# A hybrid decoder step on one core: u chunks beside the gate weights, 18 rather than 10

## The chip, the cores and the metric

One core of a Trainium2 chip runs the whole program. Its engines work side by side and wait for each other by semaphores: the matrix engine (PE), the vector engine (DVE), the activation engine (ACT), GpSimd (POOL), and SyncE (SP), which issues most transfers. The metric is the device time of one execution in microseconds; less is better.

## The reference

Two layers, a prompt of 256 tokens with 16 meta tokens ahead, and 8 samples of 4 tokens. Layer 0 mixes with RWKV-7, layer 1 with a Mamba-2 state-space part; behind each stands the same expert mixer, which the change touches most:

```python
q = (xt @ w_q).reshape(T, P_HEADS, 2, P_QDIM // 2)
s = jnp.einsum('thzd,zhkd->thzk', q, sub_keys)
sv, si = lax.top_k(s, 16)                    # two halves of a key
cand = sv[:, :, 0, :, None] + sv[:, :, 1, None, :]
top_s, pos = lax.top_k(cand.reshape(T, 8, 256), 16)
gate = jax.nn.softmax(top_s, axis=-1)        # 8 heads x 16 experts of 16384
act = gelu(einsum('td,ted->te', x_blk, u_tab[eidx]))
out = einsum('te,ted->td', gate * act, v_tab[eidx])
```

All is in float32. The outputs are the two groups' activations and the states of both mixers.

## The kernel before, in words

**The mixer (peer).** For the 256 prompt tokens the experts aren't gathered: all 16384 are computed, in 128 chunks of 128 experts, and a gate weight that is zero for an expert that wasn't chosen leaves the right ones. (The 48 or 32 other tokens do gather their rows, by indirect transfers that POOL issues in the v loop.) The tile G holds, for chunk b and token t, first gelu(u x) and then its product with the gate weight. Four stages follow each other in each layer:

1. *Queries and scores* for the keys, in tiles ti = 1, 2 (128 tokens each) and 0 (the gathered ones).
2. *The u loop*, 56 chunks (B0). s_chunk() fetches 128 x 1024 weights on SP's queue, splits them into a high part (a cast on ACT, L279) and a low part (a subtraction on POOL, L284, or on DVE, L286), and PE multiplies 24 times (mm3: L305, L306, L308) into the PSUM tile psc; ACT applies gelu (L1080) into G. Meanwhile DVE selects the best keys in topk(0), topk(1), topk(2). The table AFTER says behind which chunk the three last steps of each tile stand: exps() on ACT (L1019), gates() on DVE (L1022 to L1024), and finish(). finish() transposes the two key numbers and the gate of each choice on PE (ptk, L1029) and ACT copies them into sel (L1032).
3. *The gate stage*: 64 groups of four tokens. onehots() builds from sel two one-hot tiles oa and ob for each token, on DVE, ACT and POOL by the letters of WA; PE multiplies them (pwt, L1135), which gives the gate weights of all 16384 experts for that token. DVE multiplies them into the 56 chunks that G has (L1136), and ACT copies those of the other 72 chunks into G (L1137). Among the groups stand NF = 10 further u chunks, whose gelu goes into a scratch tile hs; at the end ten multiplies (L1139) bring hs into G.
4. *The v loop*: for each b the product of G's chunk with the v rows, 12 products into four accumulators acc (L1288), after a split of both into high and low parts (gh and glo, whi and wlo). In between the 62 u chunks that are left, each with one multiply of its own (L1252).

**What sets the order.** Both mixers stand in a block whose instructions a scheduler of the compiler lists by a simulated timeline: on each engine it may move an instruction ahead of others that it doesn't depend on, so a u chunk of stage 3 can stand far ahead of its place in the text. Calls of keep_in_program_order (in finish(), exps() and the start of gates()) hold an instruction at its place. On the chip each engine then works through its list in that order.

**The state-space part** begins with prenorm(): xh on ACT (L337), xl on DVE (L339), the squares (L315, L319), and a first projection on PE between. Ahead of it two weight tiles are split, their low halves on POOL (load_w with leng = 8), and L1340 casts a mask on DVE.

Some settings: W1 = 3 buffers of each one-hot tile; two each of whi and wlo; PSUM banks o = 4, s = 2, m = 2.

Of the kernel before, what the change touches and what calls it, by code (L numbers as in the profile page):

```python
# [23 lines left out]
F32 = mybir.dt.float32  # L24
F32R = mybir.dt.float32r
# [3 lines left out]
AF = mybir.ActivationFunctionType  # L29
# [8 lines left out]
KB = 8  # L38
# [28 lines left out]
def chain(*gens):  # L67
    for g in gens:
        yield from g
# [157 lines left out]
class K:  # L227
# [104 lines left out]

    def prenorm(self, out, h, g, xh, xl, sq, rr, tag, mid):

        nc = self.nc
        for k in range(KB):
            x = nc.scalar.activation(xh[:, k], h[:, k], AF.Copy, scale=self.vec(g, k))  # L337
            self.tc.keep_in_program_order(x)
            nc.vector.scalar_tensor_tensor(xl[:, k], h[:, k], self.vec(g, k), xh[:, k].bitcast(F32), op0=ALU.mult, op1=ALU.subtract)  # L339
        self.rmsnorm(out, h, g, sq, None, tag, rr, mid)  # L340
        return rr[1]
# [509 lines left out]
    def peer(self, l, ng):  # L851

        nc, tc, a, C, V = self.nc, self.tc, self.a, self.C, self.nc.vector
        mm = nc.tensor.matmul
        B0 = 56
        NF = 10
        W1 = 3
        FH = 10
        FL = 4
# [6 lines left out]
        raws = {i: self.fetch(a[f"wq{l}"][i]) for i in range(3)}  # L866
# [4 lines left out]
        G = gp.tile([128, 128, 256], F32, name="G")  # L871
        Gf = G.rearrange("p b t -> p (b t)")
        xh = gp.tile([128, KB, T], F32R, name="xh")
        xl = gp.tile([128, KB, T], F32R, name="xl")
# [64 lines left out]
        late = {}  # L939
# [135 lines left out]
        def s_chunk(b, dst, heng=None, leng=None, tag="s"):  # L1075

            w = self.load_w(a[f"u{l}"][b], heng=heng, leng=leng)
            p = self.bank([128, 256], "psc", tag)
            self.mm3(p, w, (xh[:, :, 48:T], xl[:, :, 48:T]))
            nc.scalar.activation(dst, p, AF.Gelu)  # L1080

# [7 lines left out]

        AFTER = ((14, 16, 55), (29, 31, 39), (46, 46, 52))  # L1090
        for b in range(B0):
# [31 lines left out]

        nf = 0
        nxt = onehots(0)
        for t0 in range(0, 256, 4):
            if nf < NF and t0 * NF >= nf * 256:
                s_chunk(B0 + nf, hs[:, nf * 256:nf * 256 + 256], heng=None if nf % 10 < FH else V, leng=FL)
                nf += 1
            oa, ob = nxt  # L1130
            if t0 < 252:
                nxt = onehots(t0 + 4)
            pw = self.bank([128, 4, 128], "pwt", "mo"[t0 // 4 % 3 > 0])
            for j in range(4):
                mm(pw[:, j], lhsT=oa[:, j], rhs=ob[:, j], start=True, stop=True)  # L1135
            V.tensor_mul(G[:, 0:B0, t0:t0 + 4], G[:, 0:B0, t0:t0 + 4], pw[:, :, 0:B0].rearrange("p t b -> p b t"))  # L1136
            nc.scalar.copy(G[:, B0:, t0:t0 + 4], pw[:, :, B0:].rearrange("p t b -> p b t"))  # L1137
        for i in range(NF):
            V.tensor_mul(G[:, B0 + i], G[:, B0 + i], hs[:, i * 256:i * 256 + 256])  # L1139

# [95 lines left out]
        def slot():  # L1236
# [6 lines left out]
            return 4 * r  # L1243

        ggen = chain(gather_u(range(ng)), gather())
        nleft = 128 - B0 - NF
        done = 0
        for b in range(128):
# [34 lines left out]
            todo = [(i, g, w) for g, w in ((gh, vhf), (gl, vhf), (gh, vlf)) for i in range(4)]  # L1283
            if b == 127:
                todo.sort(key=lambda x: x[0])
            for i, g, w in todo:
# [16 lines left out]
        for i, pt in enumerate(self.gpt):  # L1303
            hk = self.h[:, 4 * i:4 * i + 4, 0:16 * ng].rearrange("p k (g t) -> p k g t", t=16)
            V.tensor_add(hk, hk, pt.rearrange("p k (g t) -> p k g t", t=32)[:, :, 0:ng, 0:16])
        for i in range(4):
            ot = gview(100 + 2 * i, (128, 512))
            if i % 2:
                V.tensor_copy(ot, acc[i])
            else:  # L1310
                nc.scalar.copy(ot, acc[i])
            pt = self.bank([128, 4, 128], "pot", "s")
            for j in range(4):
                mm(pt[:, j], lhsT=ot[:, j * 128:(j + 1) * 128], rhs=C["eye"], is_transpose=True, start=True, stop=True)
            t0 = 48 + i // 2 * 128
            hk = self.h[:, i % 2 * 4:i % 2 * 4 + 4, t0:t0 + 128]
            V.tensor_add(hk, hk, pt)
# [3 lines left out]
    def mamba(self):  # L1321
# [17 lines left out]
        mk = pp.tile([128, 3, 128], BF, name="mk")  # L1339
        V.tensor_copy(mk[:, 2], C["eye"])  # L1340
        self.psum(i=2, G=2, f=2, t=2)
# [8 lines left out]
        done = [0]  # L1350
        pre = {b: self.load_w(a["win"][b], leng=LE, raw=raws[b]) for b in (40, 32)}
        xn = ep.tile([128, KB, T], F32, name="xn", tag="E")
        rr = ep.tile([128, 2, T], F32, name="rr", tag="E")

        def proj(blk):
# [7 lines left out]
            if done[0] == NU:  # L1363
                with tc.high_priority(offset=200):
                    for k in range(KB):
# [6 lines left out]
        ri = self.prenorm(xn, self.h, "nm1", xh, xl, ep.tile([128, KB, T], F32, name="sq", tag="E"), (rr[:, 0], rr[:, 1]), "t",  # L1372
                          lambda: first.append(proj(40)))
        gp = st.enter_context(tc.tile_pool(name="mg", bufs=2, reuse_waits="tile"))
# [34 lines left out]
        def decays(dp):  # L1409
# [310 lines left out]
```

## Time and profile before

| what | us |
|---|---|
| median of 3 runs (lowest, highest) | 2630.28 (2629.93, 2636.83) |
| the profiled execution; its span | 2634.19; 2632.3 |
| busy PE / DVE / ACT / POOL in the span | 2478 / 1899 / 1254 / 1008 |
| layer 0: u loop, gate stage, v loop (from, to) | 485-678, 678-785, 785-1328 |
| layer 1: u loop, gate stage, v loop | 1760-1967, 1967-2075, 2075-2622 |

In the rows of the profile an instruction is named by its line, engine, operation, and output<-inputs; the brackets give how long the engine stood idle before it and what ended that. PE's products are pipelined, so the time from one start to the next is their price, not the length printed. The rows of windows give the stretch, then busy time and count for PE, PE's weight loads, DVE, ACT and POOL (or for the engine asked alone), then the granted PE clock (1.00 is full), the share of the DMA engines, and GB/s.

### The profile page before, as it was taken

To read this page: it belongs to the slowest core of one execution; us is meant where nothing else is said; L and a number is where in the kernel's file an instruction comes from. 1 tells how busy PE (TensorE), PEld (TensorE's weight loads), DVE (VectorE), ACT (ScalarE), POOL (GpSimd) and SP (SyncE) were. 2 spreads that over 40 slices of the span, in tenths; PEclk is the share of its full clock that TensorE was granted. 3 is DMA by queue.
4 is the path that set the end of the run, shared out by engine and by line. 5 is a ranking of instruction groups with operands and counts; after the bars stand their busy time and mean duration, and the time that the engine had idled before them with its cause. 6 is when DMAs were issued, how large, how long until landed. Compare 5 with 4: busy or idle time off the path is not lost. (4 is left out here: it accounts for less than half of the span.)

```text
span 2632.3 us, 47459 instructions
## 1 busy us (share of the span) xinstructions
PE 2477.9 (94%) x18281; PEld 2137.4 (81%) x18281; DVE 1898.8 (72%) x3724; ACT 1253.6 (48%) x2384; POOL 1008.2 (38%) x863
## 2 busy tenths in 40 slices
PE   7999999996989999999978988999889899999998
PEld 4677768996978888888864886989789788888886
DVE  5355556797695678788784887769949756776777
ACT  3322223453784444444456543335448644444444
POOL 4111110495980233533146555117769401223210
PEclk9999999998999999999989999999989999999999
DMA  3111115453416788888732443555543267787774
GB/s 142 51 45 50 47 55 170 141 183 121 134 40 215 250 312 309 299 306 299 273 110 80 156 164 118 160 177 154 168 122 98 84 213 257 255 285 268 261 265 157
DMA packets 125858, 460.34 MB, mean 175 GB/s; under 512 B 14816, under 2 KB 15744, under 8 KB 122432
## 3 DMA queue, kind: packets, MB, share of 16 engines
q1 hardware_dynamic: 99488, 360.75, 42.1%
q0 software_dynamic: 26144, 96.56, 10.2%
q8 instruction: 144, 2.36, 0.4%
q14 instruction: 82, 0.67, 0.1%
HBM read 440.70 MB, written 16.56 MB: 174 GB/s over the span
## 5 line engine op out<-in xcount | busy, mean ns | idle before, releaser
L279 ACT CAST whi<-wraw 128x1024 fp32r<-128x1024 f32 (+1 forms) x619 | 642.1, 1038 | 870.7 <-PE acc L1288 312.9
L286 DVE TENSOR_TENSOR wlo<-wraw,whi 128x1024 fp32r<-128x1024 f32 (+1 forms) x493 | 593.7, 1204 | 397.2 <-ACT whi L279 339.6
L305 PE MATMUL psc<-xh,whi 128*128 128x256 f32 x2048 | 506.6, 285 | 3.1 <-ACT h L1080 2.6
L306 PE MATMUL psc<-xl,whi 128*128 128x256 f32 x2048 | 504.8, 283 | 0.0
L284 POOL TENSOR_TENSOR wlo<-wraw,whi 128x1024 fp32r<-128x1024 f32 (+1 forms) x150 | 355.1, 2374 | 176.5 <-ACT whi L279 91.0
L305 PEld LDWEIGHTS psc<-xh,whi 128*128 128x128 f32 x2048 | 388.0, 189 | 10.0 <-ACT h L1080 3.1
L306 PEld LDWEIGHTS psc<-xl,whi 128*128 128x128 f32 x2048 | 388.6, 190 | 5.5
L1066 POOL DMA_INDIRECT G<-in_un,gi x80 | 114.5, 1432 | 468.5 <-DVE glo L286 304.6
L1288 PE MATMUL acc<-whi,glo 128*128 128x512 f32 x1024 | 285.1, 399 | 6.7 <-DVE glo L286 6.7
L308 PE MATMUL psc<-xh,wlo 128*128 128x256 f32 x2048 | 290.3, 283 | 0.0
L1288 PE MATMUL acc<-whi,gh 128*128 128x512 f32 x1024 | 283.9, 398 | 1.9 <-ACT gh L279 1.0
L1288 PE MATMUL acc<-wlo,gh 128*128 128x512 f32 x1024 | 281.8, 397 | 0.0
L308 PEld LDWEIGHTS psc<-xh,wlo 128*128 128x128 f32 x2048 | 263.0, 188 | 0.5 <-issue 0.3
L1288 PEld LDWEIGHTS acc<-whi,glo 128*128 128x128 f32 x1024 | 193.8, 190 | 54.8 <-DVE glo L286 7.6
L1288 PEld LDWEIGHTS acc<-wlo,gh 128*128 128x128 f32 x1024 | 192.7, 189 | 47.8 <-DVE wlo L286 1.3
L1163 POOL DMA_INDIRECT G<-in_v,gi x80 | 117.0, 1463 | 298.2 <-DVE G L1158 163.8
L1288 PEld LDWEIGHTS acc<-whi,gh 128*128 128x128 f32 x1024 | 185.0, 189 | 40.3 <-ACT whi L279 1.6
L1135 PE MATMUL pwt<-ob,oa 128*128 128x128 f32 x1024 | 144.8, 282 | 11.6 <-DVE ob L1109 7.8
L1135 PEld LDWEIGHTS pwt<-ob,oa 128*128 128x128 f32 x1024 | 127.8, 191 | 23.2 <-issue 19.3
L305 PE MATMUL pi<-xh,whi 128*128 128x304 f32 (+1 forms) x328 | 102.5, 331 | 11.7 <-ACT xh L279 3.7
L286 DVE TENSOR_TENSOR glo<-G,gh 128x256 fp32r<-128x256 f32 x256 | 106.9, 419 | 2.7 <-ACT gh L279 2.7
L279 ACT CAST gh<-G 128x256 fp32r<-128x256 f32 x256 | 101.8, 399 | 11.7 <-PE acc L1288 11.6
(484 smaller groups left out, 4444.0 us busy)
## 6 DMA issues: line engine op xcount, KB each, us to landing
wraw<-in_u SPq DMA_DIRECT2D x256, 512.0 KB
wraw<-in_v SPq DMA_DIRECT2D x256, 512.0 KB
wraw<-in_win SPq DMA_DIRECT2D x41, 512.0 KB
wraw<-in_wq SPq DMA_DIRECT2D x32, 512.0 KB
wraw<-in_rkv SPq DMA_DIRECT2D x24, 512.0 KB
h<-in_ssm SPq DMA_DIRECT2D x8, 1024.0 KB
out_sssm<-h POOLq DMA_DIRECT2D x8, 1024.0 KB
wraw<-in_wo SPq DMA_DIRECT2D x8, 512.0 KB
```

Source lines behind the costliest of these rows:

```text
L279: self.nc.scalar.copy(hi, x)
L284: self.nc.gpsimd.tensor_sub(lo[:, :n], x[:, :n], hi[:, :n].bitcast(F32))
L286: self.nc.vector.tensor_sub(lo[:, n:], x[:, n:], hi[:, n:].bitcast(F32))
L305: nc.tensor.matmul(ps, lhsT=whi[:, k], rhs=xhi[:, x0 + k], start=start and k == 0, stop=False)
L306: nc.tensor.matmul(ps, lhsT=whi[:, k], rhs=xlo[:, x0 + k], start=False, stop=False)
L308: nc.tensor.matmul(ps, lhsT=wlo[:, k], rhs=xhi[:, x0 + k], start=False, stop=stop and k == kb - 1)
L1066: nc.gpsimd.indirect_dma_start(out=rows, out_offset=None, in_=a[f"un{l}"], in_offset=bass.IndirectOffsetOnAxis(ap=gi[:, 0, g, m:m + 1], ax ...
L1135: mm(pw[:, j], lhsT=oa[:, j], rhs=ob[:, j], start=True, stop=True)
L1163: nc.gpsimd.indirect_dma_start(out=rows, out_offset=None, in_=vrows, in_offset=bass.IndirectOffsetOnAxis(ap=gi[:, 1, g, m:m + 1], axis=0))
L1288: mm(acc[i], lhsT=g[:, t0:t0 + 128], rhs=w[:, d0:d0 + 512], start=b == 0 and g is gh and w is vhf, stop=b == 127 and w is vlf)
```

## The change

- **NF is 18.** Chunks 56 to 73 stand in the gate stage and 54 are left for the v loop. A chunk that stands before token t0 writes gelu for the tokens below t1 = t0 + 8 into hs, and for the others straight into its place in G (two activations). When the loop comes to t1, a DVE multiply (the join, L1141) brings the hs part into G, and from there on the chunk is one of the nb columns that DVE multiplies in each group (L1149); ACT copies the rest (L1150).
- **AFTER** moves finish(1) from chunk 39 to 52, exps(2) and gates(2) from 46 to 45, and finish(2) from 52 to 55.
- **The end of the v loop**: the products of b = 126 are kept and issued with those of b = 127, sorted by accumulator, in layer 0 in the order 0, 2, 1, 3.
- **The start of the state-space part**: the two low halves go to DVE, behind xl (lows()), and the mask's cast moves to a later place on DVE.

```diff
-    def prenorm(self, out, h, g, xh, xl, sq, rr, tag, mid):
+    def prenorm(self, out, h, g, xh, xl, sq, rr, tag, mid, then=None):
...
+        if then is not None:
+            then()
         self.rmsnorm(out, h, g, sq, None, tag, rr, mid)
...
-        NF = 10
+        NF = 18
...
-            nc.scalar.activation(dst, p, AF.Gelu)
+            for d, c in dst if isinstance(dst, tuple) else ((dst, slice(0, 256)),):
+                if c.start < c.stop:
+                    nc.scalar.activation(d, p[:, c], AF.Gelu)
...
-        AFTER = ((14, 16, 55), (29, 31, 39), (46, 46, 52))
+        AFTER = ((14, 16, 55), (29, 31, 52), (45, 45, 55))
...
         for t0 in range(0, 256, 4):
             if nf < NF and t0 * NF >= nf * 256:
-                s_chunk(B0 + nf, hs[:, nf * 256:nf * 256 + 256], heng=None if nf % 10 < FH else V, leng=FL)
+                t1 = min(t0 + 8, 256)
+                t = hs[:, nf % 10 * 256:nf % 10 * 256 + t1]
+                s_chunk(B0 + nf, ((t, slice(0, t1)), (G[:, B0 + nf, t1:], slice(t1, 256))), leng=FL)
+                late.append((t1, B0 + nf, t))
                 nf += 1
+            if late and late[0][0] <= t0:
+                t1, b, t = late.pop(0)
+                V.tensor_mul(G[:, b, 0:t1], G[:, b, 0:t1], t)
+                nb = b + 1
...
-            V.tensor_mul(G[:, 0:B0, t0:t0 + 4], G[:, 0:B0, t0:t0 + 4], pw[:, :, 0:B0].rearrange("p t b -> p b t"))
-            nc.scalar.copy(G[:, B0:, t0:t0 + 4], pw[:, :, B0:].rearrange("p t b -> p b t"))
-        for i in range(NF):
-            V.tensor_mul(G[:, B0 + i], G[:, B0 + i], hs[:, i * 256:i * 256 + 256])
+            V.tensor_mul(G[:, 0:nb, t0:t0 + 4], G[:, 0:nb, t0:t0 + 4], pw[:, :, 0:nb].rearrange("p t b -> p b t"))
+            nc.scalar.copy(G[:, nb:, t0:t0 + 4], pw[:, :, nb:].rearrange("p t b -> p b t"))
+        for t1, b, t in late:
+            V.tensor_mul(G[:, b, 0:t1], G[:, b, 0:t1], t)
...
-            if b == 127:
-                todo.sort(key=lambda x: x[0])
+            if b == 126:
+                kept = todo
+                todo = []
+            elif b == 127:
+                todo = sorted(kept + todo, key=lambda x: ORD.index(x[0]))
...
-        pre = {b: self.load_w(a["win"][b], leng=LE, raw=raws[b]) for b in (40, 32)}
+        pre = {}
+        for b in (40, 32):
+            pre[b] = tuple(self.wp.tile([128, KB, 128], F32R, name=n, tag=n) for n in ("whi", "wlo"))
+            nc.scalar.copy(pre[b][0], raws[b])
+        def lows():
+            for b in (40, 32):
+                tc.keep_in_program_order(V.tensor_sub(pre[b][1], raws[b], pre[b][0].bitcast(F32)))
```

**How the order moves.** Line numbers of the changed kernel are up to 15 higher. First ACT in the u loop of layer 0, around the first copy of sel (L1032, now L1033). Before it stands behind the gelu of chunk 39:

```order
L279 CAST whi<-wraw 128x1024
L1080 ACTIVATE G<-psc 128x256
L1032 COPY sel<-ptk 128x3x128
L1114 ACTIVATE oa<-cp,sel 128x128 x5
L1115 ACTIVATE oa<-oa,sel 128x128 x3
L279 CAST whi<-wraw 128x1024
```

and now behind that of chunk 52, with the second copy close to it:

```order
L1083 ACTIVATE G<-psc 128x256
L1033 COPY sel<-ptk 128x3x128
L1117 ACTIVATE oa<-cp,sel 128x128 x5
L1118 ACTIVATE oa<-oa,sel 128x128 x3
L279 CAST whi<-wraw 128x1024
L1118 ACTIVATE oa<-oa,sel 128x128 x2
L1083 ACTIVATE G<-psc 128x256
L279 CAST whi<-wraw 128x1024
L1083 ACTIVATE G<-psc 128x256
L279 CAST whi<-wraw 128x1024
```

Thirteen chunks, their casts and their gelus, moved ahead of the copy, as on PE ahead of the transposes.

Next DVE at the end of the gate stage and the first b of the v loop. Before:

```order
L1118 TENSOR_SCALAR ob<-cp,sel 128x128 x2
L1120 TENSOR_SCALAR oa<-cp,sel 128x128
L1136 TENSOR_TENSOR G<-G,pwt 128x56x4 x3
L286 TENSOR_TENSOR wlo<-wraw,whi 128x1024
L1139 TENSOR_TENSOR G<-G,h 128x256 x10
L286 TENSOR_TENSOR glo<-G,gh 128x256 x3
```

and now:

```order
L1121 TENSOR_SCALAR ob<-cp,sel 128x128 x2
L1123 TENSOR_SCALAR oa<-cp,sel 128x128
L1141 TENSOR_TENSOR G<-G,h 128x236
L1149 TENSOR_TENSOR G<-G,pwt 128x73x4 x2
L1149 TENSOR_TENSOR G<-G,pwt 128x74x4
L1141 TENSOR_TENSOR G<-G,h 128x252
L1266 TENSOR_TENSOR G<-G,h 128x256
L286 TENSOR_TENSOR glo<-G,gh 128x256 x3
```

The ten multiplies of 256 columns ahead of the three lower halves glo are gone; one join and one multiply of a v-loop chunk stand there, and the other joins stand among the groups, each some 3.5 groups behind the last.

More of the change, by code (lines that the diff above doesn't have):

```diff
@@ L855, in peer @@
         B0 = 56
-        NF = 10
+        NF = 18
         W1 = 3
-        FH = 10
         FL = 4
@@ L1124, in peer @@
         nf = 0
+        nb = B0
+        late = []
         nxt = onehots(0)
@@ L1243, in slot @@
             return 4 * r
+        ORD = (0, 1, 2, 3) if last else (0, 2, 1, 3)
         ggen = chain(gather_u(range(ng)), gather())
@@ L1305, in peer @@
             V.tensor_add(hk, hk, pt.rearrange("p k (g t) -> p k g t", t=32)[:, :, 0:ng, 0:16])
-        for i in range(4):
+        for n, i in enumerate(ORD):
             ot = gview(100 + 2 * i, (128, 512))
-            if i % 2:
+            if n % 2:
                 V.tensor_copy(ot, acc[i])
@@ L1339, in mamba @@
         mk = pp.tile([128, 3, 128], BF, name="mk")
-        V.tensor_copy(mk[:, 2], C["eye"])
         self.psum(i=2, G=2, f=2, t=2)
@@ L1372, in mamba @@
         ri = self.prenorm(xn, self.h, "nm1", xh, xl, ep.tile([128, KB, T], F32, name="sq", tag="E"), (rr[:, 0], rr[:, 1]), "t",
-                          lambda: first.append(proj(40)))
+                          lambda: first.append(proj(40)), lows)
         gp = st.enter_context(tc.tile_pool(name="mg", bufs=2, reuse_waits="tile"))
@@ L1418, in decays @@
             tc.keep_in_program_order(V.tensor_copy(mk[:, 0:2], nm))
+            V.tensor_copy(mk[:, 2], C["eye"])
             p = xs
```

## The prediction

> **What bounds the kernel now.** I read first which waits stop the matrix engine (PE), in the view of waits for PE alone (who waited, for whom, us in total, times, longest).
>
> ```profile
> PE ptk L1029 <- DVE G L1024: 20.5, 2, 10.2
> PE ptk L1029 <- DVE G L1016: 19.3, 2, 9.8
> ...
> PE acc L1288 <- DVE glo L286: 6.7, 2, 3.4
> ```
>
> Three rows hold 46.5 us, at the same two places in both layers: the transposes ptk of finish(), and the start of the v loop. The timeline of PE shows the first place in layer 0, then in layer 1.
>
> ```profile
> 607.37 0.27 PE L1029 MATMUL ptk<-c,G 128*128 128x128 f32 x1
> 617.43 0.47 PE L1029 MATMUL ptk<-c,G 128*128 128x128 f32 x1 [9.80 <-DVE G L1016]
> 628.15 0.47 PE L1029 MATMUL ptk<-c,G 128*128 128x128 f32 x1 [10.24 <-DVE G L1024]
> 628.27 0.56 PE L305 MATMUL psc<-xh,whi 128*128 128x256 f32 x1
> ...
> 631.83 1.13 PE L308 MATMUL psc<-xh,wlo 128*128 128x256 f32 x8
> ...
> 1897.95 0.33 PE L1029 MATMUL ptk<-c,G 128*128 128x128 f32 x1 [3.01 <-DVE G L1017]
> 1907.79 0.47 PE L1029 MATMUL ptk<-c,G 128*128 128x128 f32 x1 [9.51 <-DVE G L1016]
> 1918.49 0.48 PE L1029 MATMUL ptk<-c,G 128*128 128x128 f32 x1 [10.23 <-DVE G L1024]
> ```
>
> PE stands 20.0 us in layer 0 and 22.75 us in layer 1 in front of u chunk 40, because the selection on the vector engine (DVE) isn't done. Two chunks of the u loop from before the stall give the price of a chunk, 597.86 - 595.00 = 2.86 us, and 0.119 us for each of its 24 products:
>
> ```profile
> 595.00 1.11 PE L308 MATMUL psc<-xh,wlo 128*128 128x256 f32 x8
> ...
> 597.86 1.11 PE L308 MATMUL psc<-xh,wlo 128*128 128x256 f32 x8
> ```
>
> Behind the stall the first 16 products took 631.83 - 628.27 = 3.56 us, not 16 x 0.119 = 1.9. The windows say why: the granted clock (the last three figures are clock, DMA share and GB/s) had fallen to 0.50. So each stall costs 1.65 us more.
>
> ```profile
> 617.00:628.00 11.00, 0.47 (x1) 0.18 (x1) 10.96 (x13) 0.00 (x0) 0.00 (x0) 0.50 0.00 0
> ...
> 2300.00:2500.00 200.00, 200.00 (x1145) 174.31 (x1144) 143.18 (x188) 96.31 (x143) 52.94 (x34) 1.00 0.79 270
> ```
>
> The last row is the v loop: PE is busy all the time at full clock, and whatever PE work leaves it shortens it. The stage between, gate weights, is read from two windows of 26 us, all engines (PE, PEld, DVE, ACT, POOL), and the multiplies of L1136 alone, one for each group of four tokens.
>
> ```profile
> 700.00:726.00 26.00, 25.90 (x226) 25.73 (x225) 25.64 (x63) 22.40 (x66) 25.64 (x29) 1.00 0.34 103
> 745.00:771.00 26.00, 23.32 (x160) 19.94 (x160) 26.00 (x80) 25.14 (x80) 26.00 (x31) 1.00 0.01 2
> ...
> 700.00:726.00 26.00, 5.57 (x15) 1.00 0.34 103
> 745.00:771.00 26.00, 7.46 (x20) 1.00 0.01 2
> ...
> L286 DVE TENSOR_TENSOR wlo<-wraw,whi x4: 680/680/696, 701.7 to 721.2; 128x512 fp32r<-128x512 f32 x4
> ```
>
> DVE is full in both. Without chunks a group takes 26/20 = 1.30 us. In the first window 15 groups and four chunks (the four L286) pass, so a chunk stretches the stage by (26 - 15 x 1.30)/4 = 1.63 us. The density there, 3.75 groups for a chunk, is nearly that of the change, 64/18 = 3.56.
>
> **Term A: finish() moves.** finish(1) goes from behind chunk 39 to behind chunk 52, finish(2) from 52 to 55. Removed, at most: 20.0 + 22.75 of waits and 2 x 1.65 of half clock, 46.1 us. PE now reaches ptk 13 chunks later, 13 x 2.86 = 37.2 us: at 644.6 in layer 0 and, from 1897.95 - 3.01 = 1894.9, at 1932.1 in layer 1. DVE had the last operand at 628.1 and 1918.5. But it had it in a quiet time: during the stall GpSimd (POOL) has no subtractions (0.00 in the window above). In the u loop it has one of 2.40 us for each chunk (the last row), and DVE pays:
>
> ```profile
> 582.69 1.89 DVE L986 TENSOR_TENSOR G<-G 128x64 f32<-128x64 f32 x1
> ...
> 585.97 3.43 DVE L1007 TENSOR_TENSOR G<-G 128x1920 bf16<-128x1920 bf16 x1
> ...
> 608.31 3.96 DVE L1011 TENSOR_TENSOR G<-G,cp 128x2048 bf16<-128x2048 f32 x1
> ...
> 613.65 0.27 DVE L999 TENSOR_TENSOR G<-G 128x128 f32<-128x128 f32 x1
> ...
> 620.49 1.22 DVE L1007 TENSOR_TENSOR G<-G 128x1920 bf16<-128x1920 bf16 x1
> ...
> 604.93 2.40 POOL L284 TENSOR_TENSOR wlo<-wraw,whi 128x1024 fp32r<-128x1024 f32 x1 [0.24 <-ACT whi L279]
> ```
>
> The same L1007 takes 3.43 us beside POOL and 1.22 alone. From 582.69 to 608.31 the twelve two-input operations and casts cost 15.6 us over their quiet durations, 1.3 each (an estimate; between 0 and 2.2). Behind the old stall's start, 11 such operations lie ahead of ptk's last operand in layer 0 and 14 in layer 1: 628.1 + 14.3 = 642.4, ahead of PE's 644.6; 1918.5 + 18.2 = 1936.7, 4.6 us behind 1932.1. I also charge 1.4 us a layer for the first one-hots, which DVE made during the quiet time and now makes just before they are used. A = -(46.1 - 4.6 - 2.8) = -38.7 us; ends -46 (no slowing) and -21 (2.2 each: 7.7 and 17 us late). The gates of ti = 2 move from chunk 46 to 45; ACT's exponential needs DVE's L999, done at 613.9 before, and stands at 607.4 + 6 x 2.86 = 624.6, so it costs nothing while L999 is less than 10 us late; later than that, all casts behind it on ACT wait. Behind ptk on PE wait chunks 53 to 55, and the gate stage waits for them; ACT's copy of sel is what the one-hots on all engines wait for.
>
> **Term B: eight u chunks a layer leave the v loop for the gate stage.** The v loop gives up 8 x 2.86 = 22.9 us. Their loads on SP's queue move with them, into windows with a DMA share of 0.34 and 0.01. The gate stage gains 8 x 1.63 = 13.0 (bounds 0.68, DVE's half of the subtraction alone, and 2.86, PE's full price). DVE also multiplies each of 18 chunks once by 8 to 252 columns, 130 on average:
>
> ```profile
> L1139 DVE TENSOR_TENSOR G<-G,h 128x256 f32<-128x256 f32 x20 | 6.9, 420 | 0.0
> ```
>
> by that 0.42 for 256, about 0.24 each, 4.3 us. The group multiply grows from 56 to 74 columns, 36 elements on average; by L1136's 375 ns for 224 at most 0.06 each, I take 0.04, 2.4 us in 64 groups. ACT's activation of a chunk splits in two; in the first window ACT has 26 - 22.4 = 3.6 us free for four chunks, 0.9 each, which hides a second start; without that cover it would be up to 0.9 x 18 on the stage. Growth: 19.7 us. In the order on PE chunk 56 ends one group after its join, but 57 to 59 end two to six groups before theirs and the others seven to nine, so I charge no wait.
>
> Then the handover. Before, ten multiplies stand on DVE ahead of the first lower half glo, and PE waits (timeline of PE; one row of the chain of waits, for the pace of these products at full clock, 5.60/24 = 0.233 us; timeline of DVE):
>
> ```profile
> 785.02 1.20 PE L1288 MATMUL acc<-whi,gh 128*128 128x512 f32 x4 [0.50 <-ACT gh L279]
> 789.59 2.07 PE L1288 MATMUL acc<-whi,glo 128*128 128x512 f32 x4 [3.37 <-DVE glo L286]
> ...
> 794.87 1.48 PE L1288 MATMUL acc<-whi,glo 128*128 128x512 f32 x4
> ...
> 2093.18 5.60 PE acc L1288 x24
> ...
> 785.76 3.44 DVE L1139 TENSOR_TENSOR G<-G,h 128x256 f32<-128x256 f32 x10
> 789.11 1.09 DVE L286 TENSOR_TENSOR glo<-G,gh 128x256 fp32r<-128x256 f32 x3
> ```
>
> Behind the wait 12 products take 794.87 - 789.59 = 5.28 us, against 12 x 0.233 = 2.8. Now one join and one multiply stand there, under 0.9 us. I take 3.4 - 0.4 + 2.5, with half a us for the fourth slow group: 6.0 us saved a layer; ends 0 and 6.9. B = 2 x (-22.9 + 19.7 - 6.0) = -18.4; ends 2 x (-22.9 + 12.1 - 6.9) = -35 and 2 x (-22.9 + 29.6) = +13.
>
> **Term C: the ends and the start of the state-space part.** There DVE's cast and the first xl wait beside POOL's two subtractions, and PE waits for xl:
>
> ```profile
> 1336.18 0.62 PE L306 MATMUL pi<-xl,whi 128*128 128x304 f32 x1 [3.83 <-DVE xl L339]
> ...
> 1331.56 2.01 DVE L1340 CAST mk<-c 128x128 bf16<-128x128 f32 x1
> 1333.49 5.75 DVE L339 SCALAR_TENSOR_TENSOR xl<-h,vecs,xh 128x304 fp32r<-128x304 f32 x8
> ...
> 1331.13 4.67 POOL L284 TENSOR_TENSOR wlo<-wraw,whi 128x1024 fp32r<-128x1024 f32 x2
> ...
> 2620.80 2.48 DVE L1299 TENSOR_TENSOR G<-G,acc 128x512 f32<-128x512 f32 x4 [0.63 <-PE acc L1288]
> ```
>
> The cast leaves, so xl starts 1.9 us sooner, and without POOL beside it, which ran 1331.13 + 4.67 - 1333.49 = 2.3 us into it. The two subtractions come onto DVE behind xl: 2 x 1.36, twice the 0.68 for half of one. For the squares behind them 1.9 + 2.3 - 2.7, about 1.5 at best, I take 1.0. Sorting the last 24 products of the v loop frees accumulators sooner; at the kernel's end DVE is the bound (it idles 0.63 us before the first sum, last row), so 0.5 there and 0.7 in layer 0, where copies follow. C = -2.2; ends -6 and +3 (PE waiting for the kept chunk's weights).
>
> **Sum.** -38.7 - 18.4 - 2.2 = -59.3 us. The profiled execution took 2634.19 us (span 2632.3), so 2574.9; the median of the three runs is 3.9 lower, which gives 2571.0. I say 2571.
>
> **The rivals.** *DVE is late (chance 0.15).* Each two-input operation waits for a whole POOL subtraction, 2.2 us as L1007 did, the new place of finish(1) doesn't clear it, and A gives 21: 2571 + 18 = 2589. For it: L1007 paid 3.43 - 1.22 = 2.2; against: three of the twelve paid nothing. "SBUF — State Buffer" of the Trainium skill, section "Who interferes with whom", speaks for this rival: what starts first holds the shared ports for its whole instruction and the other blocks; the rows agree that some wait the whole, and none shows who started first in the changed order.
>
> *The gate stage is full (0.12).* PE is busy 25.90 of 26 in the first window; if it is the bound there, a chunk costs 2.86 rather than 1.63, B gives 2 x (-22.9 + 22.9 + 6.7 - 6.0) = +1.4, and the time is 2591. Against it: busy is modelled for pipelined products.
>
> *Better than forecast (0.07).* A is had in full, 7 more, and a chunk costs only DVE's 0.68, 2 x 8 x 0.95 = 15 less: 2571 - 22 = 2549.
>
> *Slower than before (0.05).* The join puts DVE's multiply behind a chunk's activation. If PE comes late, each of 36 joins waits for a chunk in full, 2.86 + 0.4 = 3.3 us: 2571 + 119 = 2690. It decides from 59/36 = 1.6 us a join; the lead in the order speaks against. That the change doesn't move the chunks is excluded by the order.
>
> **How the numbers follow.** The forecast has 0.61, with its own range 2553 to 2589. The range that should hold 8 in 10 reaches into the first two rivals: 2549 to 2604. Differences under 0.3% (8 us) can't be told from none. Faster needs under 2622: all but the slow rival and a part of the second's tail: 0.91; same 0.04; slower 0.05.
>
> **What would show it.** Right: no wait at ptk over 4 us; the clock at full there; 16 or so DVE operations stretched; the gate stage, first multiply to first acc product, some 20 us longer than 105; the v loop 23 us shorter; no wait of acc for glo over 1 us. Wrong: ptk waiting 8 us or more, joins that wait for ACT, or a stage longer by 30.

## The result

The changed kernel takes 2568.24 us (median of 4 runs, 2565.21 to 2571.80) beside 2631.51 us of the kernel before (2629.93 to 2636.83): the ratio is 0.9757, with a 95% interval of 0.9737 to 0.9776. Forecast were 2571 us. Its profiled execution took 2569.31 us, with a span of 2567.5 us against 2632.3.

The waits that stopped PE before, 39.8 us at ptk and 6.7 us at the start of the v loop, are gone but for a rest. The view of waits for PE, first one row of the kernel before, then the changed kernel (who waited, for whom, us in total, times, longest). Line numbers shift by more than the 15 named above: L1288 of the kernel before is L1306 now, and in the state-space part L1494 is L1520.

```profile
PE pwt L1135 <- DVE ob L1109: 7.8, 31, 1.3
```


```profile
PE pwt L1148 <- DVE ob L1121: 8.7, 11, 3.0
...
PE pwt L1148 <- DVE ob L1112: 4.9, 6, 1.5
PE ptk L1030 <- DVE G L1025: 4.1, 2, 2.7
```

No row of acc waiting for glo is left. The largest rest is pwt waiting for the one-hot tile ob. That wait was there before, in short pieces; now it is 8.7 + 4.9 = 13.6 us in 17 waits, with single ones up to 3.0. PE's timeline in layer 0 shows what is left at ptk, and the longest wait for ob:

```profile
645.65 0.38 PE L1030 MATMUL ptk<-c,G 128*128 128x128 f32 x2
647.40 0.33 PE L1030 MATMUL ptk<-c,G 128*128 128x128 f32 x1 [1.37 <-DVE G L1025]
...
658.38 1.82 PE L1148 MATMUL pwt<-ob,oa 128*128 128x128 f32 x10 [3.04 <-DVE ob L1121]
```

What DVE does at that time, by its timeline of the changed kernel:

```profile
613.34 1.03 DVE L1000 TENSOR_TENSOR G<-G 128x128 f32<-128x128 f32 x1
614.30 3.41 DVE L1016 TENSOR_TENSOR G<-G 128x2048 bf16<-128x2048 bf16 x1
617.63 2.43 DVE L998 CAST G<-G 128x128 f32<-128x128 uint32 x1
619.99 2.27 DVE L1017 TENSOR_REDUCE G<-G 128x128 f32<-128x2048 bf16 x1
...
627.47 3.41 DVE L1008 TENSOR_TENSOR G<-G 128x1920 bf16<-128x1920 bf16 x1
...
637.99 2.51 DVE L1010 SCALAR_TENSOR_TENSOR G<-G 128x128 f32<-128x128 f32 x1
640.42 0.19 DVE L1024 RECIPROCAL G<-G 128x8 f32<-128x8 f32 x1
640.53 4.44 DVE L1012 TENSOR_TENSOR G<-G,cp 128x2048 bf16<-128x2048 f32 x1
644.89 2.45 DVE L1025 TENSOR_TENSOR G<-G 128x128 f32<-128x128 f32 x1
...
653.46 2.37 DVE L1025 TENSOR_TENSOR G<-G 128x128 f32<-128x128 f32 x1
655.76 0.68 DVE L1112 TENSOR_TENSOR ob<-cp,sel 128x512 f32<-128x512 f32 x1
```

And GpSimd, with a subtraction for each u chunk (the view of L284 from 606 to 656 us: shortest, median and longest in ns, first and last start):

```profile
L284 POOL TENSOR_TENSOR wlo<-wraw,whi x16: 2387/2442/4304, 604.6 to 653.3; 128x1024 fp32r<-128x1024 f32 x16
```

Beside them, an operation of 0.28 us takes 2.5 and one of 1.22 takes 3.41; the reduction takes 2.27 as before. The last operand of ptk is ready at 644.89 + 2.45 = 647.3, and behind it the gates of the next tile stand on DVE until 655.8, ahead of the first one-hots, for which PE then waits.

The gate stage is denser and longer. The views of the two lines that mark its start and its end, kernel before (the DVE multiplication, then the first form of the v products):

```profile
L1136 DVE TENSOR_TENSOR G<-G,pwt x64: 371/375/386, 679.8 to 783.8; 128x224 f32<-128x224 f32 x64
...
L1288 PE MATMUL acc<-whi,gh x512: 389/394/628, 785.0 to 1326.6; 128*128 128x512 f32 x171
```

The same two of the changed kernel, and then three windows (the second overlaps the first; PE, PE's loads, DVE, ACT, POOL, then clock, DMA share, GB/s):

```profile
L1149 DVE TENSOR_TENSOR G<-G,pwt x64: 380/413/451, 664.9 to 784.9; 128x228 f32<-128x228 f32 x4, 128x232 f32<-128x232 f32 x4, 128x240 f32<-128x240 f32 x4, 128x248 f32<-128x248 f32 x4
...
L1306 PE MATMUL acc<-whi,gh x512: 388/394/498, 786.1 to 1302.9; 128*128 128x512 f32 x171
```

```profile
640.00:660.00 20.00, 15.59 (x127) 15.06 (x127) 19.90 (x17) 10.82 (x23) 18.20 (x16) 0.99 0.47 154
645.00:665.00 20.00, 15.59 (x116) 15.06 (x116) 18.07 (x21) 9.95 (x22) 18.51 (x18) 0.91 0.41 128
...
700.00:720.00 20.00, 19.09 (x163) 18.68 (x162) 20.00 (x51) 16.38 (x51) 18.80 (x20) 1.00 0.26 79
```

First multiplication to first v product: 785.0 - 679.8 = 105.2 us before and 786.1 - 664.9 = 121.2 now; first to last v product 541.6 and 516.8. (The last v product is here the last of whi and gh, as in the rows above; the very last one starts 1.1 to 2.3 us later in these runs.) With such marks, taken in the profile of every run, the program falls into stretches. The u loop goes from its first product to the first gate multiplication; "between" is from layer 0's last v product to layer 1's first u product. us, layer 0 / layer 1:

| kernel | u loop | gate stage | v loop | between |
|---|---|---|---|---|
| before | 194.2 / 197.1 | 105.2 / 105.2 | 541.6 / 544.2 | 446.4 |
| changed | 179.7 / 180.1 | 121.2 / 121.4 | 516.8 / 517.6 | 432.0 |
| e1 list order | 174.7 / 180.2 | 105.7 / 105.3 | 541.3 / 544.9 | 448.0 |
| e2 mamba start | 194.1 / 197.0 | 105.3 / 105.2 | 543.9 / 546.2 | 433.7 |
| e3 ends | 194.1 / 197.5 | 105.2 / 105.3 | 541.5 / 543.5 | 445.4 |
| e4 18 chunks | 194.7 / 195.6 | 120.7 / 120.9 | 517.1 / 518.9 | 446.7 |
| e5 no POOL subtraction | 169.7 / 170.1 | 119.1 / 119.0 | 521.5 / 517.6 | 434.1 |
| e6 10 chunks, joined | 179.5 / 175.6 | 108.6 / 109.2 | 538.4 / 538.7 | 432.3 |
| e7 26 chunks | 179.6 / 176.0 | 138.3 / 139.0 | 498.7 / 495.0 | 432.2 |
| e8 subtractions later | 194.7 / 197.0 | 105.7 / 105.2 | 542.4 / 544.1 | 442.6 |
| e9 subtraction on DVE | 195.7 / 197.8 | 115.5 / 115.6 | 517.5 / 517.6 | 439.4 |
| e10 34 chunks | 179.7 / 180.5 | 157.1 / 157.1 | 477.0 / 473.3 | 437.7 |
| e11 unit matrix later | 194.7 / 197.1 | 105.3 / 105.3 | 544.9 / 544.5 | 449.0 |
| e12 26 chunks, casts on ACT | 203.3 / 205.4 | 138.8 / 139.0 | 498.0 / 494.4 | 434.7 |

So the 64.8 us of the span came from the u loops, -14.5 and -17.0; from gate stage and v loop, +16.0 - 24.8 and +16.2 - 26.6; from the stretch between, -14.4. The kernel's end grew by 0.7 by this mark; from the very last v product it is 11.2 us in both kernels. The rest lies ahead of layer 0's u loop.

### The profile page after: what moved, and what is told of

It reads as the page before. It is cut to its first block, busy times and chain, and to the rows that moved or that the text cites. A ratio compares the mean times of both kernels' runs of the same rounds, so it can differ in the third digit from the quotient of the medians.

```text
span 2567.5 us, 47546 instructions
## 1 busy us (share of the span) xinstructions
PE 2457.1 (96%) x18281; PEld 2123.9 (83%) x18281; DVE 1927.6 (75%) x3726; ACT 1239.9 (48%) x2414; POOL 1042.1 (41%) x877
## 4 chain that ended last, share of the span: by engine, by line
PE 57%; DVE 22%; DMA 2%; ACT 2%; issue 1%; POOL 1%; DVEq 0%; ACTq 0%; SPq 0%; POOLq 0%
PE acc L1306 27%; PE psc L308 5%; PE psc L305 5%; PE psc L306 5%; PE pwt L1148 3%; DVE G L984 1%; DVE wlo L286 1%; DVE ob L1112 1%; PE pq L306 1%; DVE ac L1419 1%; PE pq L305 1%; DMA wraw<-in_v 1%; PE pi L306 1%; PE pq L308 1%; PE pi L305 1%
## 5 line engine op out<-in xcount | busy, mean ns | idle before, releaser
L286 DVE TENSOR_TENSOR wlo<-wraw,whi 128x1024 fp32r<-128x1024 f32 (+1 forms) x493 | 580.5, 1178 | 349.0 <-ACT whi L279 288.4
L284 POOL TENSOR_TENSOR wlo<-wraw,whi 128x1024 fp32r<-128x1024 f32 (+1 forms) x164 | 388.3, 2376 | 165.2 <-ACT whi L279 106.0
L1306 PE MATMUL acc<-whi,gh 128*128 128x512 f32 x1024 | 282.6, 396 | 4.9 <-ACT gh L279 2.7
L1067 POOL DMA_INDIRECT G<-in_un,gi x80 | 110.2, 1378 | 434.7 <-DVE glo L286 282.0
L1306 PE MATMUL acc<-whi,glo 128*128 128x512 f32 x1024 | 283.0, 396 | 0.0
L1306 PE MATMUL acc<-wlo,gh 128*128 128x512 f32 x1024 | 280.1, 395 | 0.2 <-DVE wlo L286 0.2
L1306 PEld LDWEIGHTS acc<-wlo,gh 128*128 128x128 f32 x1024 | 191.5, 188 | 49.1 <-issue 1.7
L1306 PEld LDWEIGHTS acc<-whi,glo 128*128 128x128 f32 x1024 | 192.2, 188 | 46.9 <-issue 0.9
L1306 PEld LDWEIGHTS acc<-whi,gh 128*128 128x128 f32 x1024 | 184.7, 188 | 44.0 <-ACT gh L279 3.5
L1120 POOL TENSOR_SCALAR oa<-cp,sel 128x128 f32<-128x128 f32 x128 | 105.0, 830 | 6.9 <-PE pwt L1148 3.1
```

Source lines behind the costliest of these rows:

```text
L284: self.nc.gpsimd.tensor_sub(lo[:, :n], x[:, :n], hi[:, :n].bitcast(F32))
L286: self.nc.vector.tensor_sub(lo[:, n:], x[:, n:], hi[:, n:].bitcast(F32))
L1067: nc.gpsimd.indirect_dma_start(out=rows, out_offset=None, in_=a[f"un{l}"], in_offset=bass.IndirectOffsetOnAxis(ap=gi[:, 0, g, m:m + 1], ax ...
L1120: nc.gpsimd.tensor_scalar(oa[:, j], C["iota"], sel[:, 0, t:t + 1], None, op0=ALU.is_equal)
L1306: mm(acc[i], lhsT=g[:, t0:t0 + 128], rhs=w[:, d0:d0 + 512], start=b == 0 and g is gh and w is vhf, stop=b == 127 and w is vlf)
```

## The experiments

**The four parts, each alone.** If the change is four independent edits, each should bring its stretch and the four should add up.

```diff
-        AFTER = ((14, 16, 55), (29, 31, 39), (46, 46, 52))
+        AFTER = ((14, 16, 55), (29, 31, 52), (45, 45, 55))
```

> The kernel before with one line changed: the table that says after which u chunk each part of the list work stands is the changed kernel's; gate stage (10 chunks), mamba start and kernel end as before. Theory (the two traces): the change saved 31.9 us between the first u chunk and the first gate multiplication (14.5 and 17.0 us by layer), so this alone gives 2631.5 - 32 = 2600 us, with a list transposition that waits some 1 to 3 us and no multiplication-free stretch longer than 4 us there. Prediction on record: 38.7 us, 2593 us. Rival that the rest of the change (the mamba start lies ahead of layer 1's u chunks) helped here: under 25 us, over 2606 us.

Measured: 2598.48 us beside 2633.18, ratio 0.9859 (0.9834 to 0.9883): the theory, and close to the prediction on record too. (14.5 and 17.0 are 31.5; the 31.9 of the expectation is a slip.) The two u loops became 19.5 and 16.9 us shorter. Layer 0 is the better one, with neither wait. Its DVE timeline shows two small operations that weren't held up:

```profile
636.24 0.28 DVE L1009 SCALAR_TENSOR_TENSOR G<-G 128x128 f32<-128x128 f32 x1
...
649.46 0.29 DVE L1024 TENSOR_TENSOR G<-G 128x128 f32<-128x128 f32 x1
```

In the changed kernel the same two took 2.51 and 2.37 us. While the second ran, GpSimd was at a one-hot and not at a subtraction (its timeline, e1):

```profile
648.93 0.82 POOL L1120 TENSOR_SCALAR oa<-cp,sel 128x128 f32<-128x128 f32 x1
```

Such a difference of 4.3 us, from how the two engines happen to fall against each other, is about what PE waits in the changed kernel's layer 0, 1.4 + 3.0 us. That the one makes the other is argued from these rows; no run varies it alone.

```diff
-        V.tensor_copy(mk[:, 2], C["eye"])
...
-        pre = {b: self.load_w(a["win"][b], leng=LE, raw=raws[b]) for b in (40, 32)}
+        pre = {}                      # high halves on ACT here, lows() on DVE behind xl
...
+            V.tensor_copy(mk[:, 2], C["eye"])
```

> The kernel before with the edits at the start of the state-space layer alone: the two weight subtractions behind the eight shifted subtractions of the norm, and the copy of the unit matrix behind the mask. Theory: the 14.4 us by which the stretch from layer 0's last v product to layer 1's first u chunk is shorter come from these edits, because the instructions behind them stand in another order: 2617 us, exponentials grouped, fewer table loads on ScalarE. Rival, the prediction on record: 1.7 us, 2630 us; the other 12.7 us then come from what layer 0's v loop leaves behind (gathers, stores, the last copies).

Measured: 2625.06 us beside 2633.18, ratio 0.9961 (0.9942 to 0.9979). The stretch between is 433.7 us, 12.7 shorter, in this one profile; by the runs the edits are worth 8 to 10 us. Either is several times the 1.0 us that the prediction put on this start (the 1.7 of the expectation takes in 0.7 for the sorted products, which this run doesn't have).

```diff
-            if b == 127:
-                todo.sort(key=lambda x: x[0])
+            if b == 126:
+                kept = todo
+                todo = []
+            elif b == 127:
+                todo = sorted(kept + todo, key=lambda x: ORD.index(x[0]))
```

> The kernel before with only the end of the v loop changed: the products of chunk 126 held back and sorted with those of 127 by output bank, and the copies out in the new order. Theory: nothing that can be told from no change, 2631 us (2629 to 2634): the kernel's end was 0.7 us longer in the changed kernel, and the stretch behind layer 0 is to be paid for by the mamba edits. Rival: this is where the 14.4 us behind layer 0 come from, since the first addition to the token rows starts earlier: 2617 us.

Measured: 2632.09 us beside 2633.18, ratio 0.9993 (0.9978 to 1.0008), between 445.4 us: nothing that can be told from no change, as the theory had it, and not where the 14.4 us come from.

```diff
-        NF = 10
+        NF = 18
...
+            if late and late[0][0] <= t0:
+                t1, b, t = late.pop(0)
+                V.tensor_mul(G[:, b, 0:t1], G[:, b, 0:t1], t)
+                nb = b + 1
```

> The kernel before with the gate stage of the changed kernel alone: 18 u chunks beside the gate weights with their joins, 8 fewer in the v loop; the list order, mamba start and kernel end as before. Theory: B of the prediction and the traces' 19.2 us: 2612 us, gate stage 16 us longer per layer, v loop 25 us shorter. Rival: chunks and list order depend on each other (the gate stage starts 10 to 15 us nearer to the one-hots' first inputs), so this alone is worth under 12 us or over 26 us, and the four parts do not add up to 63 us.

Measured: 2613.75 us beside 2633.18, ratio 0.9916 (0.9897 to 0.9936); gate stage 120.7 and 120.9, v loops 517.1 and 518.9. The theory. The four medians add up to -34.7 - 8.1 - 1.1 - 19.4 = -63.3 us, and the change made 2631.51 - 2568.24 = 63.3; the four ratios multiply to 0.9731, just below the lower edge of the change's interval. The parts are independent within what these runs can tell.

**What makes DVE late.** The prediction blamed GpSimd's subtractions for each slow operation on DVE. The test takes them away for the chunks during which the list work ends. It leaves out the low half of these chunks' weights; PE multiplies the high half in its place, with as many instructions.

```diff
+            if 40 <= b < B0:
+                raw = self.fetch(a[f"u{l}"][b])
+                hi = self.wp.tile([128, KB, 128], F32R, name="whi", tag="whi")
+                nc.scalar.copy(hi, raw)
+                w = (hi, hi)
+            else:
                 w = self.load_w(a[f"u{l}"][b], heng=heng, leng=leng)
```

> The changed kernel with GpSimd's subtraction left out for the u chunks 40 to 55 of each layer: their low half is taken to be the high half, so the last third part of the products of these chunks is wrong; PE's instructions are as many as before. Theory: the list operations that read two tensors on DVE (3.41 us for one that takes 1.22 alone, 2.45 for 0.29) are stretched by GpSimd's subtraction and by nothing else; without it they go back to 1.2 and 0.3, the last transposition and the first one-hots wait for nothing, and both u stages come to the 174.7 us that the list order alone had in layer 0: 5 us a layer, 2558 us. Rival 1: DVE is late for other work of its own, the operations keep their length, 2569 us. Rival 2: the one-hots' first inputs are early, but the gate stage then fills with the work put off, 2564 us.

Measured: 2549.18 us beside 2634.93, ratio 0.9670 (0.9654 to 0.9686). Against the changed kernel's 0.9757 that is some 23 us, twice what the theory said. DVE's timeline in this run, the same operations as above:

```profile
610.87 1.21 DVE L1016 TENSOR_TENSOR G<-G 128x2048 bf16<-128x2048 bf16 x1
612.01 0.41 DVE L998 CAST G<-G 128x128 f32<-128x128 uint32 x1
612.14 2.27 DVE L1017 TENSOR_REDUCE G<-G 128x128 f32<-128x2048 bf16 x1
...
622.31 0.28 DVE L1010 SCALAR_TENSOR_TENSOR G<-G 128x128 f32<-128x128 f32 x1
...
624.84 0.29 DVE L1025 TENSOR_TENSOR G<-G 128x128 f32<-128x128 f32 x1
```

The two-input operations are at their quiet lengths, the reduction at the 2.27 us that it has in both. (The cast has 0.41 us here and 2.43 above; quiet it took 0.22 in the kernel before.) DVE has ptk's operand at 625.1 instead of 647.3. This is what the Trainium skill states in "SBUF — State Buffer", section "Who interferes with whom": an instruction of DVE with two inputs in SBUF shares ports with GpSimd, and on trn2 a reduction never does. The runs agree with both halves.

The gain that the theory missed shows in windows from the first u product to the first v product, of the changed kernel and of this one:

```profile
485.20:786.10 300.90, 287.33 (x2393) 282.25 (x2391) 294.01 (x867) 194.57 (x449) 258.26 (x178) 0.99 0.44 136
```

```profile
485.30:774.10 288.80, 283.79 (x2394) 280.35 (x2392) 265.35 (x866) 193.59 (x448) 211.20 (x162) 1.00 0.46 140
```

PE has the same products. From 485 to 625 us the two kernels do the same: PE is busy in all of the 140 us, with 1188 products in either, so a full DVE costs nothing there. The 12.1 us come behind that: PE's idle time falls from 13.6 to 5.0 us, and the same products take 3.5 us less. The changed kernel's granted clock was 0.91 from 645 to 665 us, around its waits; this one's was 1.00 there. DVE is busy 294.0 of 300.9 us in the changed kernel and has 28.7 us less to do without the 16 subtractions in layer 0, 24.6 in layer 1. In the gate stage it is full in both kernels, so what it is late at the end of the u loop isn't made up there. The gate stage gained a little as well (121.2 to 119.1), where I had expected the gain to end at ptk.

If GpSimd is the trouble, the subtractions could stand on DVE, without leaving anything out:

```diff
-        LB = 200
+        LB = 40
```

> The changed kernel with the low halves of the u chunks 40 to 55 subtracted by DVE rather than by GpSimd, 16 subtractions of about 1.2 us each in a layer. Leaving GpSimd's out altogether took DVE's busy time in layer 0's u stage from 177.8 to 147.7 us and saved 12 us a layer. Theory: DVE gets the 30 us back and pays 19, so it is some 11 us less busy and the u stage and gate stage together are 3 to 5 us a layer shorter: 2561 us. Rival: the low halves now stand behind list operations of up to 4.4 us on DVE, PE waits for them, and what is saved at the end of the u stage is lost in it: 2569 us or more.

Measured: 2594.88 us beside 2634.99, ratio 0.9850 (0.9822 to 0.9878): some 24 us slower than the change, as the rival said. Waits of PE over the whole run, and DVE's timeline:

```profile
PE psc L308 <- DVE wlo L286: 44.5, 2, 23.5
```

```profile
608.02 1.21 DVE L1016 TENSOR_TENSOR G<-G 128x2048 bf16<-128x2048 bf16 x1
...
625.64 2.35 DVE L286 TENSOR_TENSOR wlo<-wraw,whi 128x1024 fp32r<-128x1024 f32 x2
```

The list operations are quiet, as the theory wanted (1.21 us again), and the gate stage is 5.7 us shorter than in the changed kernel. But the scheduler stood nearly all list operations ahead of the first subtraction on DVE; PE wanted chunk 40's low half 21.0 us before DVE had it, and 23.5 in layer 1. The u loop without that wait would be 195.7 - 21.0 = 174.7 us. Two waits, one for each layer, ate more than the whole gain.

**What a chunk costs in the gate stage.** With the joins kept, only the number of chunks is varied.

```diff
-        NF = 18
+        NF = 10        # e6; 26 in e7, 34 in e10
```

> The changed kernel with 10 chunks beside the gate weights rather than 18, joined as they come. It tells what the 8 moved chunks are worth from what the joins are worth (no row of ten multiplications between the gate stage and the first v product). Prediction on record: the 8 chunks save 3.2 us a layer (22.9 less 19.7) and the joins 6.0, so this kernel takes 2575 us. Rival: the joins are worth the 3.4 us wait and no more, the 8 chunks some 6 us a layer, 2581 us; or the chunks are worth all of 9.6 us a layer, 2588 us.

> The changed kernel with 26 chunks beside the gate weights, 8 more. From 10 to 18 the gate stage grew by 16.1 us, 2.0 us a chunk, the v loop lost 24.8. Theory: the stage is full at 18 (DVE busy 20.00 of 20 us, PE 19.1), so each further chunk costs its whole 2.86 us on PE or more, with the join and the wider multiplications on DVE: stage 121 to 147 us or more, v loop 23 us shorter, 2569 to 2580 us. Rival: the 2.0 us go on, stage 137 us, two layers save 14 to 17 us, 2553 us.

> The changed kernel with 34 chunks beside the gate weights. With 10, 18 and 26 the gate stage took 108.6, 121.2 and 138.3 us in layer 0: 1.6 and then 2.1 us a chunk; with 26 PE was busy 19.6 to 20 of 20 us in it. Theory: PE is full, so a chunk costs its 2.9 us there and saves as much in the v loop: stage 161 us, time as with 26, 2561 us (2556 to 2567). Rival: the price stays near 2.1 us and the gain goes on, 2550 us. Second rival: DVE, with wider multiplications, becomes the bound again and the time rises over 2569 us.

Measured: 10 chunks 2583.57 us, ratio 0.9810 (0.9791 to 0.9829); 26 chunks 2561.24 us, 0.9722 (0.9705 to 0.9738); 34 chunks 2559.62 us, 0.9707 (0.9682 to 0.9732). The windows 745 to 765 us into the span, of 10, 18, 26 and 34 chunks in turn:

```profile
745.00:765.00 20.00, 17.23 (x116) 14.66 (x117) 20.00 (x61) 18.33 (x59) 19.00 (x22) 1.00 0.01 2
```

```profile
745.00:765.00 20.00, 19.29 (x162) 18.58 (x161) 20.00 (x50) 16.88 (x54) 18.84 (x20) 1.00 0.26 80
```

```profile
745.00:765.00 20.00, 19.62 (x166) 19.16 (x165) 19.33 (x48) 15.93 (x48) 18.06 (x19) 1.00 0.35 107
```

```profile
745.00:765.00 20.00, 20.00 (x174) 20.00 (x173) 19.66 (x44) 16.33 (x46) 16.18 (x17) 1.00 0.37 124
```

The stage in layer 0 takes 108.6, 121.2, 138.3 and 157.1 us, so a chunk costs 1.6 us from 10 to 18, 2.1 from 18 to 26 and 2.4 from 26 to 34; a chunk taken out of the v loop saves 2.3 to 2.8. DVE is full up to 18; from 26 on PE takes over, with 174 products in 20 us at 34. By the traces each chunk still costs a little less than it saves, and the gain runs dry: 15.3, 7.0 and 1.6 us by the medians.

For 10 chunks the truth lies between the expectation on record (2575) and the rival that gave the chunks everything (2588). The 3.2 us that I took from the prediction were wrongly split: the growth of 19.7 us holds 6.7 for joins and wider multiplications, of which 10 joined chunks pay some 3.7 already (10 of 18 joins, and a width that grows by 20 elements on average rather than 36). Split so, the prediction says 22.9 - 13.0 - 3.0 = 6.9 us a layer for the eight chunks and 6.0 - 3.7 = 2.3 for joining the first ten; both are estimates. Measured: 21.6 - 12.6 = 9.0 and 21.1 - 12.2 = 8.9 for the chunks; the joins at 10 chunks +3.4 and +4.0 in the stage, -3.2 and -5.5 in the v loop, little or nothing on the whole (-0.2 and 1.5).

For 26 chunks the rival was right, in direction: I took a busy PE of 19.1 in 20 us for a full one. Both 26 and 34 chunks are faster than the changed kernel; for 34 the two intervals (0.9682 to 0.9732, 0.9737 to 0.9776) don't overlap, for 26 they just touch. The runs can't tell 34 from 26. For 34 the time lies in the theory's range, but the stage took 157.1 us and not 161.

**The start of the state-space part.** The two edits there are taken one at a time.

```diff
# e8: lows() behind xl, the copy of the unit matrix left where it was
# e11: the copy alone
-        V.tensor_copy(mk[:, 2], C["eye"])
...
+            V.tensor_copy(mk[:, 2], C["eye"])
```

> The kernel before with one of the two mamba edits: the two weight subtractions behind the norm's eight shifted subtractions; the copy of the unit matrix stays where it was. Theory: the stretch from layer 0's last v product to layer 1's first u chunk, 446.4 us before and 433.7 with both edits, becomes 434 us with this one alone, because the eight subtractions no longer stand behind two that wait for weights: 2619 to 2625 us. Rival: the copy of the unit matrix (2.01 us where it stood, 0.22 where it went) gives the gain, and the stretch stays at 446 us here: 2632 us. Half and half (440 us) would say that both count.

> The kernel before with the other of the two mamba edits: only the copy of the unit matrix moved behind the mask, the two weight subtractions where they were. The stretch from layer 0's last v product to layer 1's first u chunk took 446.4 us before, 442.6 with the subtractions moved alone, 433.7 with both. Theory: the edits act on different pieces (the copy takes 2.01 us ahead of the norm, 0.22 later), so the copy alone gives the missing 8.9 us: stretch 438 us, 2624 us. Rival: the copy matters only once the subtractions are out of the way, or the planner's order depends on both: stretch 444 to 447 us, 2633 us.

Measured: the subtractions alone 2625.12 us beside 2634.93, ratio 0.9958 (0.9943 to 0.9973), between 442.6; the copy alone 2634.88 beside 2634.99, 0.9997 (0.9987 to 1.0008), between 449.0. The runs give the copy nothing and the subtractions all that both edits had (0.9961). The single profiles split it otherwise, 3.8 us for the subtractions and 8.9 more with the copy, but they scatter: runs with the same code in this stretch (changed, e5, e6, e7, e9, e10, e12) show 432.0 to 439.4 us. I follow the runs.

What moved is in the groups of ACT, in the stretch between. Kernel before, then e8 (line, operation, count, then busy us and mean ns):

```profile
L1397 ACT ACT_TABLE_LOAD x4 | 5.1, 1283 | 0.1
L1494 ACT ACT_TABLE_LOAD x4 | 5.1, 1283 | 0.1
L1647 ACT ACT_TABLE_LOAD x3 | 3.8, 1283 | 0.1
L1603 ACT ACT_TABLE_LOAD x3 | 3.8, 1283 | 1.2 <-PE pv L1601 1.0
```

```profile
L1407 ACT ACT_TABLE_LOAD x3 | 3.8, 1283 | 0.1
L1613 ACT ACT_TABLE_LOAD x3 | 3.8, 1283 | 1.2 <-PE pv L1611 1.0
L328 ACT ACT_TABLE_LOAD x1 | 1.3, 1283 | 0.0
...
L1504 ACT ACT_TABLE_LOAD x1 | 1.3, 1283 | 0.0
```

Before there are these 14 loads of a function table and two single ones, 16; with the subtractions moved, two groups of three and four single ones, 10. Ten stand in the changed kernel too, and 16 in e11. ACT had been switching between the exponential (L1494) and the other functions; in the new order the exponentials stand together. Six loads are 7.7 us of ACT. PE's waits for the decay operands go with it, before and e8:

```profile
PE pe L1492 <- POOL rh L1489: 7.0, 3, 2.8
```

```profile
PE pe L1502 <- POOL rh L1499: 3.9, 3, 2.3
```

That the loads are the cause and not a companion wasn't tried: no run keeps the new order and puts the loads back.

**An attempt to help DVE.** Since DVE is the fullest engine there, two casts of its list work go to ACT, which is busy 10 of 20 us in the u loop.

```diff
-            V.tensor_copy(sif.rearrange("p h z k -> p (h z) k"), si)
+            nc.scalar.copy(sif.rearrange("p h z k -> p (h z) k"), si)
...
-            V.tensor_copy(posf, pos)
+            nc.scalar.copy(posf, pos)
```

> The kernel with 26 chunks, and the two casts of key numbers in the selection (L979, L998) on ACT rather than on DVE; with 26 chunks they take 5.9 and 9.4 us of DVE in the whole run, stretched by GpSimd's subtraction like the rest, so DVE gets 7.6 us a layer back and ACT, busy some 10 of 20 us there, takes them. Theory: DVE is the bound of the u loop, its end comes by the 3 to 5 us earlier a layer that PE still waits for it there: 2553 us (26 chunks alone 2561). Rival: what DVE gets back goes to waits for ACT, in whose queue the casts stand behind those of the weights: 2561 us. Second rival: PE waits for whi behind the casts on ACT: over 2565 us.

Measured: 2612.20 us beside 2636.47, ratio 0.9912 (0.9894 to 0.9931): some 50 us slower than 26 chunks without it, the second rival and far beyond it. PE's waits over the run, then the two casts in the groups of ACT:

```profile
PE psc L305 <- ACT whi L279: 42.1, 10, 7.2
```

```profile
L979 ACT CAST G<-G 128x256 bf16<-128x256 uint32 (+1 forms) x6 | 2.2, 369 | 52.9 <-DVE G L977 52.9
L998 ACT CAST G<-G 128x128 f32<-128x128 uint32 (+1 forms) x6 | 1.7, 281 | 25.0 <-DVE G L995 25.0
```

The casts themselves are cheap, 3.9 us in all. But ACT stands 77.9 us in front of them waiting for DVE, with the high halves of the weights behind it in its queue, and PE waits for those.

## Why the prediction was right

The total, -63.3 us by the medians against -59.3 forecast, is right partly because two errors cancel: by the runs alone term A gave 34.7 us rather than 38.7, and term C 9.2 rather than 2.2. That they cancel is luck.

**Term A (-38.7) was too large by 7.2.** The u loops lost 14.5 + 17.0 = 31.5 us in the changed kernel. Of the 7.2, some 4.2 were not to be had by this edit: with no wait for DVE (layer 0 of e1) the stretch is 174.7 us, so at most 19.5 + 22.4 = 41.9 us could go while GpSimd's subtractions stay, not 46.1; the price of the stalls was summed from waits and half-clock products instead of being read as a stretch. The other 3.0 are what the changed kernel lost beyond the 4.6 + 2.8 us charged: its u loops stand 5.0 and 5.4 us above 174.7. PE waited 1.4 + 2.7 = 4.1 us at ptk, about as charged, but 3.0 + 1.8 = 4.8 for the first one-hots, where 1.4 a layer were charged; some 1.5 us are left, beside a granted clock of 0.91 for which nothing was charged.

That ptk came out near its 4.6 is luck in part. The step "11 such operations, 1.3 each" was too low in layer 0. From the start of L1000 at 613.34 to the operand at 647.3 the list work took 34.0 us, against 628.1 - 613.65 = 14.4 for the same operations before: 19.6 us over 11 operations are 1.8 each. In layer 1 it was 1.4. That lies between the forecast's 1.3 and the 2.2 of the rival "DVE is late". Counted from the first u product, layer 0's operand was ready after 162.1 us rather than the forecast's 156.8, but PE came later too, after 160.8 rather than 159.0. The mechanism was the right one, as e5 shows, and the ceiling was named: ptk waits at most 2.7 us, under the 4 given. What I overlooked is that DVE's lateness doesn't end at ptk: the next tile's gates and the first one-hots stand behind it, and DVE stays full in the gate stage.

**Term B (-18.4) held.** Measured are (16.0 - 24.8) + (16.2 - 26.6) = -19.2 in the profile (-18.4 by the very last v products), and 19.4 alone in e4. Its pieces offset each other. The stage grew by 16 rather than 19.7: ten joined chunks cost the +3.4 and +4.0 that joins and wider multiplications had been charged for (some 3.7), but eight more cost 12.6 and 12.2 where 16.0 had been charged, so the chunk price of 1.63, read from two windows, was too high; 1.6 is what a chunk cost from 10 to 18 with its join and its width in it. The v loop and handover gave 24.8 and 26.6 rather than 28.9. (In the working, 64 groups of 0.04 us are 2.6 and not 2.4; that changes nothing.) Joins wait for nothing, so the slow rival never began, and "the gate stage is full" fell with e6 and e7: even between 26 and 34 the price, 2.4 us, stays under PE's 2.86.

**Term C (-2.2) is the step that failed: -14.4 in the profile, 8 to 10 in the runs of e2.** The start itself went as written. DVE's timeline of the changed kernel behind layer 0:

```profile
1307.97 0.22 DVE L1444 CAST mk<-c 128x128 bf16<-128x128 f32 x1
1308.11 3.65 DVE L339 SCALAR_TENSOR_TENSOR xl<-h,vecs,xh 128x304 fp32r<-128x304 f32 x8
1311.68 2.36 DVE L1375 TENSOR_TENSOR wlo<-wraw,whi 128x1024 fp32r<-128x1024 f32 x2
```

xl takes 3.65 us rather than 5.75, a gain of 2.1 where 2.3 were written. But I priced only the first five or six instructions and stopped there. The scheduler sets the whole state-space part by its simulated timeline, so moving two subtractions at its start also changed which function follows which on ACT much later. The order of the changed kernel was there to be read before any run, down to the table loads; the prediction looked at it in the three places where its terms were.

Of the signs named, the clock was nearly full at ptk (0.99 from 640 to 660 us, 0.93 in the 20 us behind), the wait of acc for glo is gone, and 14 operations on DVE are stretched in layer 0 between 605 and 656 us, for 16 said.

## What to carry to other kernels

Before pricing a wait away, ask which engine bounds the stretch around it: here DVE was busy 294 of 301 us over two stages, so what it was late at the end of the first couldn't be made up in the second. Read the price of a stall as the difference of stretches between fixed marks, not as a sum of waits; and where a scheduler lists the instructions, compare its whole order, since a small move at a block's start can be repaid far behind it. Moving work to an idle engine helps only if that engine needn't wait for its operands ahead of work that others want: 3.9 us of casts cost some 50 us.

## What the runs showed of the hardware

Two things had not been expected in this size. Beside GpSimd's subtraction most operations of DVE that read two tensors, and casts, took longer, by up to about the 2.4 us of one subtraction, whatever their own length: 0.28 us became 2.51, a cast of 0.22 became 2.43, 1.21 became 3.41. GpSimd gave way seldom: its 16 subtractions had a median of 2.44 us (2.39 at the shortest), and the longest took 4.30. Taken together, 16 subtractions cost DVE 28.7 us in layer 0 and 24.6 in layer 1. And ACT's alternation between functions is visible as loads of 1283 ns each, 16 in one stretch before and 10 after.
